# Partial-array matmuls alternate between row halves, column halves and quadrants, and each join step writes one bank

## The chip, the core and the metric

The kernel runs on one core of one Trainium2 chip. The metric is the device time of one execution in microseconds; lower is better. Three executions of the kernel before took 2127.93, 2128.15 and 2136.32 us, so the time before is their median, 2128.15 us.

## What is computed

The reference is one sequence of 256 tokens of width 1024 through two blocks. The first block has two layers of feed-forward, a mixer of three kinds of heads, a cross attention to a memory, and a second feed-forward. The second block has a gated delta rule over a context and then over the tokens, an attention, and a convolved feed-forward. Two places of it matter here. The RWKV heads of the mixer run a recurrence that the kernel solves in two chunks of 128 tokens:

```python
sa = jnp.einsum('bhij,bhj->bhi', state, -kk_t)
state = (state * w_t[:, :, None, :] + sa[..., None] * (kk_t * a_t)[:, :, None, :]
         + v_t[..., None] * k_t[:, :, None, :])
```

and the gated delta rule solves a triangular system per chunk:

```python
a_mat = jnp.where(strict, beta[..., :, None] * dec * kk, 0.0) + jnp.eye(GDN_CHUNK, dtype=jnp.float32)
uw = lax.linalg.triangular_solve(a_mat, rhs, left_side=True, lower=True, unit_diagonal=True)
```

Both come down to inverses of 128x128 unit triangular matrices, eight at a time. The mixer also holds two small attentions with heads of 64 (`foxmoba`), whose scores contract over 64 rows.

## The kernel before

**What fills TensorE.** Most of the program is large products in a three-term split (`xh*wh + xl*wh + xh*wl`, with `h` and `l` the rounded value and its rest). They come from `gemm_pair` (moving tiles of 256 columns) and `gemm_tok` (512 columns). Weights arrive through `raw`, ScalarE makes `wh`, VectorE makes `wl`. Every matmul is recorded on line 351, every transpose on line 354, so tiles are told apart by name.

**What runs beside them.** `merge` and `Side` interleave several generators: each `yield t` hands the turn to whichever generator is due next. In the mixer these are two RWKV groups (`rwkv` with `gi` 0 and 1), `foxmoba` and `mix_out`. During the feed-forwards after the first mixer, the context side of the delta rule (`context`) runs beside them; in the second block the token side does. A scheduler then places the instructions on each engine, mostly in the order in which they were written. TensorE takes its queue in that order as far as waits go.

**The inverse.** `inverse` (line 676) is called 12 times: 4 in the mixers (`rN`, `rW`), 4 for the context and 4 for the tokens (`gN`, `gW`, in two of the last `xv` in place of `gW`). It takes eight matrices in two halves `hf` of four. `lows` says for each half whether it is lower or upper triangular: both lower in the mixers, one of each in the delta rule. After a 16x16 stage on VectorE and a step on the whole array there are four join steps, called A to D here. A and B work on 32x32 quadrants of the array, C and D on 64x64 quarters:

- A multiplies a block of `N` with one of `T` into `Z`, 16 matmuls;
- B multiplies `Z` with `W`, 16 matmuls, and 8 more (`own`) that give the transposed block;
- C and D do the same on 64x64, 8 matmuls each.

An fp32 matmul leaves two records in the trace, so an inverse has 112 records of TensorE in A to D (80 on quadrants, 32 on quarters). Before the change, each half and each pair of blocks `(ee, oo)` has a bank of its own (`ps = e.bank()`, out of two) and an evacuation of its own, and its four matmuls on one quadrant stand in a row:

```python
for hf, (ee, oo) in eo:
    ps = e.bank()
    for j in range(4):
        u = 4 * hf + j
        s.mm(ps[qd(oo), j * 32:j * 32 + 32], N[qd(ee), u, qd(oo)], T[qd(ee), u, qd(ee)])
    s.act(Z[qd(oo), hs[hf], :32], v4(ps[qd(oo), :128]))
```

**The other places.** `scores` in `foxmoba` contracts over 64 rows, head by head, two heads per row half. In `rwkv`, `inv` makes `N` from four matmuls on the low row half and then four on the high one; `rest` makes `G` with two matmuls per head, four heads, heads alternating between row halves with a `yield 1.5` after each; the loop over chunks at its end multiplies `U` and `vt` with `G` on column halves; `values` in `foxmoba` also works on column halves.

Of the kernel before, what the change touches and what calls it, by code (L numbers as in the profile page):

```python
# [189 lines left out]
def f2(ap):  # L190
    return ap.rearrange("p a b -> p (a b)")
# [84 lines left out]
class Builder:  # L276
# [399 lines left out]
    def inverse(s, e, N, W, lows, pace=(1.0, 1.0)):  # L676
# [75 lines left out]
        for hf, (ee, oo) in eo:  # L752

            ps = e.bank()
            own = (ee < 2) == lows[hf]
            for j in range(4):
                u = 4 * hf + j
                s.mm(ps[qd(ee), j * 32:j * 32 + 32], Z[qd(oo), u, :32], W[qd(oo), u, qd(oo)])
            if own:
                for j in range(4):  # L760
                    u = 4 * hf + j
                    s.mm(ps[qd(oo), j * 32:j * 32 + 32], W[qd(oo), u, qd(oo)], Z[qd(oo), u, :32])
                nc.vector.tensor_copy(T[qd(oo), hs[hf], qd(ee)], v4(ps[qd(oo), :128]))
            s.act(W[qd(ee), hs[hf], qd(oo)], v4(ps[qd(ee), :128]))
        yield 1.5 * pace[1]

        for hf, sl in enumerate(hs):
            a, b = (slice(0, 64), slice(64, 128)) if lows[hf] else (slice(64, 128), slice(0, 64))
            ps = e.bank()
            for j in range(4):  # L770
                u = 4 * hf + j
                s.mm(ps[b, j * 64:j * 64 + 64], N[a, u, b], T[a, u, a])
            s.act(Z[b, sl, :64], v4(ps[b, :256]))
        yield 1.5 * pace[1]
        for hf, sl in enumerate(hs):
            a, b = (slice(0, 64), slice(64, 128)) if lows[hf] else (slice(64, 128), slice(0, 64))
            ps = e.bank()
            for j in range(4):
                u = 4 * hf + j
                s.mm(ps[a, j * 64:j * 64 + 64], Z[b, u, :64], W[b, u, b])  # L780
            s.act(W[a, sl, b], v4(ps[a, :256]))
        yield 1.5 * pace[1]


# [102 lines left out]
    def foxmoba(s, e, l, m):  # L887
# [32 lines left out]
        for a in range(2):  # L920
# [56 lines left out]
            def scores(qb):  # L977
                n = 128 * (qb + 1)
                sc = e.t([128, 4, 256], "fcb" if a and qb else "sc")[:, :, :n]
                for p in range(2):  # L980
                    ps = e.bank()
                    for i in range(2):
                        h = 2 * i + p
                        o = ps[:, i * n:i * n + n]
                        rw = slice(64 * p, 64 * p + 64)
                        s.mm(o, qT[rw, i, qb * 128:qb * 128 + 128], qT[rw, 2 + i, :n])
# [20 lines left out]
            def values(qb, sc):  # L1007
                PT = e.t([128, 2, 4, 128], "PT")
                for kb in range(qb + 1):
                    pt = e.bank()  # L1010
                    for h in range(4):
                        s.tr(pt[:, h * 128:h * 128 + 128], sc[:, h, kb * 128:kb * 128 + 128])
                    s.act(f2(PT[:, kb]), pt)
                yield 2.0
                po = e.bank()
                for i in range(2):
                    for p in range(2):
                        h = 2 * i + p
                        vc = slice(a * 256 + h * 64, a * 256 + h * 64 + 64)
                        o = po[64 * p:64 * p + 64, i * 128:i * 128 + 128]  # L1020
                        for kb in range(qb + 1):
# [18 lines left out]
    def rwkv(s, e, ec, l, gi, m):  # L1040
# [79 lines left out]
        def inv():  # L1120
# [1 line left out]
                yield "inv0"  # L1122
            N = t([128, 8, 128], "rN")
            nc.gpsimd.memset(N, 0.0)
            for p in range(2):
                ps = e.bank()
                rw = slice(64 * p, 64 * p + 64)
                for c in range(2):
                    cc = slice(c * 128, c * 128 + 128)
                    for ct in range(2):  # L1130
                        u = c * 2 + ct
                        s.mm(ps[:, u * 128:u * 128 + 128], nb[rw, ct, cc], E[rw, 0, ct, cc])
# [6 lines left out]
        def rest():  # L1139
# [60 lines left out]
        for c in range(2):  # L1200
# [31 lines left out]
            for ct in range(2):  # L1232
                o = ps[:, ct * 128:ct * 128 + 128]
                if c:
                    s.mm(o, SB[:, ct], E[:, 1, ct, cc], ct == 0, False)
                for pr in range(2):
                    h = 2 * ct + pr
                    hc = slice(h * 64, h * 64 + 64)
                    oo = o[64 * pr:64 * pr + 64]
                    s.mm(oo, U[:, hc], G[:, h, 0], ct == 0 and not c, False)  # L1240
                    s.mm(oo, vt[:, c, hc], G[:, h, 2], False, ct == 1)
            s.act(y[:, :, cc], v2(ps[:, :256]))
            flags.add(f"scan{gi}{c}")
            yield 2.0
# [825 lines left out]
```

## Time and profile before

| | before |
|---|---|
| median of 3 runs | 2128.15 us |
| profiled execution, its own time | 2126.08 us |
| span in the trace | 2124.3 us |
| mean granted TensorE clock | 0.97 of full speed |
| TensorE busy | 2040.3 us (96%) |
| VectorE busy | 1606.1 us (76%) |
| ScalarE busy | 1128.2 us (53%) |

The span runs from the first to the last instruction of the profiled execution; 1.8 us of its own time lie around it, and that time is 2.1 us below the median. A row of the timeline gives the start, the length from the first start to the last end, the engine, the line, the operation, the tiles it writes and reads, and how many records it merges. The end of a matmul is modelled and reaches past the start of the next one, so what a matmul costs TensorE is the distance from start to start, not its length.

### The profile page before, as it was taken

The page shows a single profiled execution, that of the slowest core. Times are in us where ns is not written, and L with a number is a line of the kernel's source. Part 1 is how long each engine was busy: PE and PEld are TensorE (multiplying, and loading weights), DVE is VectorE, ACT ScalarE, POOL GpSimd, SP SyncE. Part 2 cuts the span into 40 slices and gives each one's busy share as a digit, 9 for nine tenths or more (in the row PEclk, how much of TensorE's full clock was granted, in tenths as well). Part 3 has the DMA queues.
Part 4 walks back from the last instruction along what each step waited for, and adds up shares of the span by engine and source line. Part 5 has one row for each costly group of instructions (what it writes and reads, how often), then busy time and mean ns, then how long its engine had stood idle before and what let it go on. Part 6 is the DMA issues. An engine that isn't in the chain of part 4 may idle for free.

```text
span 2124.3 us, 37334 instructions
## 1 busy us (share of the span) xinstructions
PE 2040.3 (96%) x14344; PEld 1802.5 (85%) x14344; DVE 1606.1 (76%) x3832; ACT 1128.2 (53%) x2113; POOL 14.9 (1%) x16
## 2 busy tenths in 40 slices
PE   8999999999999999999999978999889999999998
PEld 8899887778989989898888768999678888878996
DVE  7977688477695969586698578686788787767985
ACT  6544554376454556464555355444546564546663
POOL 0000000000000000000000000000000000000000
PEclk9999999899999999999999898999989999999999
DMA  8766532154554445454432167665431123555564
GB/s 300 243 225 179 158 108 70 53 171 129 163 160 147 155 135 161 148 163 141 147 119 80 43 216 246 197 226 170 136 98 60 51 61 100 168 163 166 197 191 129
DMA packets 90570, 317.18 MB, mean 149 GB/s; under 512 B 10388, under 2 KB 12952, under 8 KB 90008
## 3 DMA queue, kind: packets, MB, share of 16 engines
q1 hardware_dynamic: 90392, 314.80, 46.7%
q8 instruction: 112, 1.84, 0.4%
q14 instruction: 66, 0.54, 0.1%
HBM read 313.72 MB, written 1.05 MB: 148 GB/s over the span
## 4 chain that ended last, share of the span: by engine, by line
PE 78%; DVE 15%; ACT 3%; issue 2%; DMA 1%; SPq 0%; ACTq 0%; DVEq 0%
PE b L351 75%; DVE wl L327 4%; PE b L354 4%; ACT wh L324 1%; DVE iv_x L348 1%; DVE macc L345 1%; DVE iv_tz L701 1%; DVE iv_p L327 1%; DMA wm<-in_wmod_dram 1%; DVE gcv L345 1%; ACT sq L324 1%; ACT iv_c L324 0%; DVE sg L327 0%; DVE iv_tz L327 0%; DVE gW L327 0%
## 5 line engine op out<-in xcount | busy, mean ns | idle before, releaser
L324 ACT ACTIVATE wh<-raw 128x1024 fp32r<-128x1024 f32 (+1 forms) x546 | 568.9, 1043 | 602.6 <-PE b L351 443.1
L327 DVE TENSOR_TENSOR wl<-raw,wh 128x1024 fp32r<-128x1024 f32 (+1 forms) x546 | 654.2, 1201 | 266.1 <-ACT wh L324 234.4
L351 PE MATMUL b<-xTh,wh 128*128 128x256 f32 x2200 | 625.7, 285 | 2.9 <-ACT xTh L324 2.4
L351 PE MATMUL b<-xTh,wl 128*128 128x256 f32 x2200 | 621.1, 283 | 1.2 <-DVE wl L327 1.2
L351 PE MATMUL b<-xTl,wh 128*128 128x256 f32 x2200 | 620.4, 283 | 0.3 <-DVE xTl L345 0.2
L351 PEld LDWEIGHTS b<-xTh,wh 128*128 128x128 f32 x2200 | 416.6, 190 | 8.5 <-ACT xTh L324 3.9
L351 PEld LDWEIGHTS b<-xTh,wl 128*128 128x128 f32 x2200 | 417.6, 190 | 3.6 <-DVE wl L327 1.9
L351 PEld LDWEIGHTS b<-xTl,wh 128*128 128x128 f32 x2200 | 417.7, 190 | 3.1 <-DVE xTl L345 1.3
L351 PE MATMUL b<-wh,gh 128*128 128x512 f32 x440 | 176.0, 400 | 0.2 <-DVE gcv L345 0.2
L351 PE MATMUL b<-wl,gh 128*128 128x512 f32 x440 | 174.5, 397 | 0.2 <-DVE wl L327 0.2
L351 PE MATMUL b<-wh,gl 128*128 128x512 f32 x440 | 173.8, 395 | 0.0
L351 PE MATMUL b<-wh,xTh 128*128 128x512 f32 x400 | 163.1, 413 | 6.3 <-DVE iv_x L348 5.0
L351 PE MATMUL b<-wl,xTh 128*128 128x512 f32 x400 | 163.8, 411 | 0.3 <-DVE wl L327 0.3
L351 PE MATMUL b<-wh,xTl 128*128 128x512 f32 x400 | 162.4, 407 | 0.0
L351 PEld LDWEIGHTS b<-wl,gh 128*128 128x128 f32 x440 | 83.5, 190 | 18.6 <-DVE wl L327 0.6
L351 PEld LDWEIGHTS b<-wh,gh 128*128 128x128 f32 x440 | 83.5, 190 | 18.3 <-ACT wh L324 0.6
L351 PEld LDWEIGHTS b<-wh,gl 128*128 128x128 f32 x440 | 83.5, 190 | 17.3
L351 PEld LDWEIGHTS b<-wh,xTh 128*128 128x128 f32 x400 | 76.4, 192 | 25.4 <-issue 8.6
L351 PEld LDWEIGHTS b<-wl,xTh 128*128 128x128 f32 x400 | 76.9, 192 | 19.7 <-issue 4.0
L351 PEld LDWEIGHTS b<-wh,xTl 128*128 128x128 f32 x400 | 77.0, 192 | 15.6 <-issue 1.0
L345 DVE SCALAR_TENSOR_TENSOR macc<-wm,mcs,macc 128x512 f32<-128x512 f32 x112 | 82.6, 747 | 0.8 <-DMA wm<-in_wmod_dram 0.3
L324 ACT ACTIVATE iv_tz<-b 32x128 f32<-32x128 f32 (+2 forms) x96 | 31.1, 325 | 62.0 <-PE b L351 58.2
(608 smaller groups left out, 3181.3 us busy)
## 6 DMA issues: line engine op xcount, KB each, us to landing
raw<-in_f1i_dram SPq DMA_DIRECT2D x88, 512.0 KB, 3.8
raw<-in_f2i_dram SPq DMA_DIRECT2D x88, 512.0 KB, 4.2
wm<-in_wmod_dram SPq DMA_DIRECT2D x48, 512.0 KB, 4.8
raw<-in_wup_dram SPq DMA_DIRECT2D x44, 512.0 KB, 4.4
raw<-in_f1o_dram SPq DMA_DIRECT2D x40, 512.0 KB, 3.7
raw<-in_wi_q_dram SPq DMA_DIRECT2D x40, 512.0 KB, 3.8
raw<-in_f2o_dram SPq DMA_DIRECT2D x40, 512.0 KB, 3.7
raw<-in_wi_a_dram SPq DMA_DIRECT2D x32, 512.0 KB, 3.9
```

The costliest lines, as they stand in the source:

```text
L324: return s.nc.scalar.activation(out, in_, func, scale=scale, bias=bias, **kw)
L327: return s.nc.vector.tensor_tensor(out, a, b, op=op)
L345: return s.nc.vector.scalar_tensor_tensor(out, a, sc, b, op0=op0, op1=op1)
L348: s.nc.vector.tensor_reduce(out, in_, axis=AX.X, op=op)
L351: s.last_mm = s.nc.tensor.matmul(out, lhsT, rhs, start=start, stop=stop).ins
L354: s.nc.tensor.transpose(out, in_, s.c("ident"))
L701: nc.vector.stream_shuffle(AR[:, j, :, j:], NC[:, :, j:], [j] * 16 + [16 + j] * 16)
```

## The change

The matmuls of A to D are written in another order: the loop over `j` is outside, so that neighbours in the queue stand on different quadrants or quarters, and a whole step writes one bank. `alike` is true in the mixers, where both halves use the same quadrants and the second half then takes other columns of the bank. In the delta rule the halves use different quadrants and share columns. Fewer, larger evacuations follow: step A has 2 instead of 4 (`alike`) or 1, step C has 1 instead of 2. `own` of step B gets a bank apart. `N`, `G`, `scores`, the products with `G` and `values` alternate in the same way, with their banks as before; `G` goes by pairs of heads with a `yield 3.0`.

```diff
-        for hf, (ee, oo) in eo:
-            ps = e.bank()
-            for j in range(4):
-                u = 4 * hf + j
-                s.mm(ps[qd(oo), j * 32:j * 32 + 32], N[qd(ee), u, qd(oo)], T[qd(ee), u, qd(ee)])
-            s.act(Z[qd(oo), hs[hf], :32], v4(ps[qd(oo), :128]))
+        alike = lows[0] == lows[1]
+        co = lambda hf, w: 4 * w * hf if alike else 0
+        ps = e.bank()
+        for j in range(4):
+            for hf, (ee, oo) in eo:
+                u, c = 4 * hf + j, co(hf, 32) + 32 * j
+                s.mm(ps[qd(oo), c:c + 32], N[qd(ee), u, qd(oo)], T[qd(ee), u, qd(ee)])
+        if alike:
+            for oo in sorted({oo for _, (_, oo) in eo}):
+                s.act(Z[qd(oo), :, :32], ps[qd(oo), :256].rearrange("p (a b) -> p a b", a=8))
+        else:
+            s.act(Z[:, :4, :32], v4(ps[:, :128]))
...
+        own = [(hf, q) for hf, q in eo if (q[0] < 2) == lows[hf]]
+        ps = e.bank()
+        for j in range(4):
+            for hf, (ee, oo) in eo:
+                u, c = 4 * hf + j, co(hf, 32) + 32 * j
+                s.mm(ps[qd(ee), c:c + 32], Z[qd(oo), zu(hf, j), :32], W[qd(oo), u, qd(oo)])
+        po = e.bank()
+        for j in range(4):
+            for hf, (ee, oo) in own:
+                u, c = 4 * hf + j, co(hf, 32) + 32 * j
+                s.mm(po[qd(oo), c:c + 32], W[qd(oo), u, qd(oo)], Z[qd(oo), zu(hf, j), :32])
...
+        ps = e.bank()
+        for j in range(4):
+            for hf, (a, b) in enumerate(ab):
+                u, c = 4 * hf + j, co(hf, 64) + 64 * j
+                s.mm(ps[b, c:c + 64], N[a, u, b], T[a, u, a])
...
+                pp = [e.bank() for _ in range(2)]
+                for i in range(2):
+                    for p in range(2):
+                        rw = slice(64 * p, 64 * p + 64)
+                        s.mm(pp[p][:, i * n:i * n + n], qT[rw, i, qb * 128:qb * 128 + 128], qT[rw, 2 + i, :n])
...
-                for h in range(4):
-                    ct, rw = h // 2, slice(64 * (h % 2), 64 * (h % 2) + 64)
-                    ps = ec.bank()
-                    s.mm(ps[:, :128], nb[rw, ct, cc], E[rw, 1, ct, cc])
-                    s.mm(v2(ps[:, 128:384]), kt[rw, ct, cc], E[rw, 0:2, ct, cc])
-                    nc.vector.copy_predicated(f2(G[:, h]), s.uc[:, 640:1024], ps[:, :384])
-                    yield 1.5
+                for ct in range(2):
+                    pp = [(ec.bank(), slice(64 * p, 64 * p + 64)) for p in range(2)]
+                    for ps, rw in pp:
+                        s.mm(ps[:, :128], nb[rw, ct, cc], E[rw, 1, ct, cc])
+                    for ps, rw in pp:
+                        s.mm(v2(ps[:, 128:384]), kt[rw, ct, cc], E[rw, 0:2, ct, cc])
+                    for p, (ps, rw) in enumerate(pp):
+                        nc.vector.copy_predicated(f2(G[:, 2 * ct + p]), s.uc[:, 640:1024], ps[:, :384])
+                    yield 3.0
```

What this does to the queue of TensorE is shown at three places. First, steps A and B of the first context inverse, before (`gN` is `N`, `gW` is `W`, `iv_tz` holds `T` and `Z`; the `128x256` rows are the large product that fills the time, one of several each time):

```order
L351 MATMUL b_7046<-iv_tz,gN 32x32 x4
L351 MATMUL b_7052<-iv_tz,gN 32x32 x4
L351 MATMUL b_7070<-xTh,wh 128x256
...
L351 MATMUL b_7058<-iv_tz,gN 32x32 x4
L351 MATMUL b_7064<-iv_tz,gN 32x32 x4
...
L351 MATMUL b_7101<-gW,iv_tz 32x32 x4
L351 MATMUL b_7101<-iv_tz,gW 32x32 x4
L351 MATMUL b_7112<-gW,iv_tz 32x32 x4
...
L351 MATMUL b_7118<-gW,iv_tz 32x32 x4
L351 MATMUL b_7070<-xTl,wh 128x256
L351 MATMUL b_7124<-gW,iv_tz 32x32 x4
L351 MATMUL b_7124<-iv_tz,gW 32x32 x4
```

and the same two steps on TensorE after the change:

```order
L351 MATMUL b_7018<-iv_tz,gN 32x32 x16
L351 MATMUL b_7036<-xTh,wh 128x256
L351 MATMUL b_7036<-xTl,wh 128x256
...
L351 MATMUL b_7036<-xTh,wl 128x256
L351 MATMUL b_7067<-gW,iv_tz 32x32 x16
L351 MATMUL b_7084<-iv_tz,gW 32x32 x8
```

Five stretches of quadrant matmuls became two; between A and B stand 24 matmuls of the large product, and C and D (not shown) are one stretch of 8 matmuls each, as they were. Second, TensorE in the first mixer where the inverse of the second RWKV group joins, before (`rE`, `ra`, `rzk` belong to `G`, `wl` and `wh` with `xTh` to the large product):

```order
L351 MATMUL b_4073<-iv_tz,rN 32x32 x4
L351 MATMUL b_4135<-rE,ra 128x128
L351 MATMUL b_4079<-iv_tz,rN 32x32 x4
L351 MATMUL b_4135<-rE,rzk 128x256
L351 MATMUL b_4085<-iv_tz,rN 32x32 x4
L351 MATMUL b_4091<-iv_tz,rN 32x32 x4
L351 MATMUL b_4152<-wl,xTh 128x512
L351 MATMUL b_4152<-wh,xTh 128x512
L351 MATMUL b_4101<-rW,iv_tz 32x32 x4
L351 MATMUL b_4101<-iv_tz,rW 32x32 x4
```

and after (`rG`, `rU`, `rvt`, `rSB` are the products with `G` at the end of the first group):

```order
L351 MATMUL b_4059<-iv_tz,rN 32x32 x14
L351 MATMUL b_4115<-rG,rvt 64x128
L351 MATMUL b_4115<-rE,rSB 128x128
L351 MATMUL b_4115<-rG,rU 64x128
L351 MATMUL b_4086<-rW,iv_tz 32x32
L351 MATMUL b_4115<-rG,rU 64x128
L351 MATMUL b_4115<-rG,rvt 64x128
L351 MATMUL b_4086<-rW,iv_tz 32x32 x15
L351 MATMUL b_4103<-iv_tz,rW 32x32 x8
```

The join steps are now whole, and less of the large product stands between them. Third, `scores` over 256 keys on TensorE in the first mixer, before (two banks, `b_4451` and `b_4456`, one for each row half):

```order
L351 MATMUL b_4451<-qkT 128x256
L351 MATMUL b_4456<-qkT 128x256
L351 MATMUL b_4462<-wl,xTh 128x512
L351 MATMUL b_4463<-wh,xTl 128x512
L351 MATMUL b_4451<-qkT 128x256
L351 MATMUL b_4487<-fconst,rE_3111 128x2
L351 MATMUL b_4456<-qkT 128x256
```

and after:

```order
L351 MATMUL b_4423<-qkT 128x256
L351 MATMUL b_4424<-qkT 128x256
L351 MATMUL b_4423<-qkT 128x256
L351 MATMUL b_4424<-qkT 128x256
L351 MATMUL b_4459<-fconst,rE_3111 128x2 x4
```

The four matmuls of the scores now follow each other. Over the whole program, TensorE's 12552 matmuls are the same ones; neighbours that differ in the part of the array they use in size (whole, half, quarter, quadrant) are 380 pairs before and 318 after.

## Rows read from the trace of the kernel before

**Rows 1.** The page: span, busy time by engine, the chain by engine.
```profile
span 2124.3 us, 37334 instructions
...
PE 2040.3 (96%) x14344; PEld 1802.5 (85%) x14344; DVE 1606.1 (76%) x3832; ACT 1128.2 (53%) x2113; POOL 14.9 (1%) x16
...
PE 78%; DVE 15%; ACT 3%; issue 2%; DMA 1%; SPq 0%; ACTq 0%; DVEq 0%
```

**Rows 2.** Stretches: length, busy by engine (records), granted clock, DMA share, GB/s.
```profile
300.00:445.00 145.00, 142.97 (x1020) 110.52 (x1019) 96.26 (x266) 67.21 (x157) 3.72 (x3) 0.93 0.25 82
640.00:1005.00 365.00, 357.18 (x2975) 333.73 (x2974) 274.42 (x640) 194.46 (x363) 0.00 (x0) 0.99 0.48 150
...
1580.00:1800.00 220.00, 211.73 (x1703) 188.83 (x1703) 173.14 (x600) 123.78 (x301) 0.00 (x0) 0.93 0.21 66
```

**Rows 3.** Stretches of single inverses, PE's `iv_tz` matmuls alone; last: all twelve.
```profile
368.70:388.10 19.40, 8.28 (x112) 0.53 0.04 6
...
651.00:668.00 17.00, 4.86 (x112) 1.00 0.53 170
...
1653.00:1667.00 14.00, 6.54 (x112) 0.76 0.24 77
...
sum 189.00, PE 71.92; mean PE 5.99
```

**Rows 4.** Timeline, PE: four matmuls on one quadrant, between large ones.
```profile
309.36 0.28 PE L351 MATMUL b<-xTh,wh 128*128 128x256 f32 x1
309.56 0.43 PE L351 MATMUL b<-iv_tz,rN 32*32 32x32 f32 x8
309.93 0.39 PE L351 MATMUL b<-xTl,wh 128*128 128x256 f32 x1
310.15 0.28 PE L351 MATMUL b<-xTh,wl 128*128 128x256 f32 x1
```

**Rows 5.** Timeline, PE: half of step A, two quadrants in two banks.
```profile
653.00 0.28 PE L351 MATMUL b<-xTh,wl 128*128 128x256 f32 x1
653.21 0.59 PE L351 MATMUL b<-iv_tz,gN 32*32 32x32 f32 x16
653.73 0.39 PE L351 MATMUL b<-xTh,wh 128*128 128x256 f32 x1
```

**Rows 6.** Timeline, PE: step C, two quarters in two banks.
```profile
662.77 0.28 PE L351 MATMUL b<-xTl,wh 128*128 128x256 f32 x1
662.89 0.28 PE L351 MATMUL b<-xTh,wl 128*128 128x256 f32 x1
663.10 0.96 PE L351 MATMUL b<-iv_tz,gN 64*64 64x64 f32 x16
```

**Rows 7.** Timeline, PE: start of step B.
```profile
655.31 0.34 PE L351 MATMUL b<-gW,iv_tz 32*32 32x32 f32 x5
655.46 0.21 PE L351 MATMUL b<-iv_tz,gW 32*32 32x32 f32 x1
655.49 0.19 PE L351 MATMUL b<-gW,iv_tz 32*32 32x32 f32 x1
```

**Rows 8.** Timeline, PE: `G`, two heads that stand together, then one alone.
```profile
328.07 0.50 PE L351 MATMUL b<-rE,ra 64*128 64x128 f32 x4
328.39 0.61 PE L351 MATMUL b<-rE,rzk 64*128 64x256 f32 x4
...
331.86 0.49 PE L351 MATMUL b<-rE,ra 64*128 64x128 f32 x2
332.19 0.59 PE L351 MATMUL b<-rE,rzk 64*128 64x256 f32 x2
```

**Rows 9.** Timeline, PE: `N` of the first group, two row halves.
```profile
266.98 1.71 PE L351 MATMUL b<-rE,ra 64*128 64x128 f32 x16
```

**Rows 10.** Timeline, PE: scores over 256 keys, both halves, then one.
```profile
419.22 0.70 PE L351 MATMUL b<-qkT 64*128 64x256 f32 x4
...
420.52 0.70 PE L351 MATMUL b<-qkT 64*128 64x256 f32 x2
```

More of the change, by code (lines that the diff above doesn't have):

```diff
@@ L765, in inverse @@
-        yield 1.5 * pace[1]
[L767 to L773, printed above, removed]
-        yield 1.5 * pace[1]
[L775 to L781, printed above, removed]
+        alike = lows[0] == lows[1]
@@ new lines, in inverse @@
+        zu = lambda hf, j: 4 * hf + j if alike else j
+        yield 1.5 * pace[1]
+        own = [(hf, q) for hf, q in eo if (q[0] < 2) == lows[hf]]
[9 more added lines that the diff above has]
+                s.mm(po[qd(oo), c:c + 32], W[qd(oo), u, qd(oo)], Z[qd(oo), zu(hf, j), :32])
@@ new lines, in inverse @@
+        if alike:
+            for hf, (ee, oo) in own[:1]:
+                nc.vector.tensor_copy(T[qd(oo), :, qd(ee)], po[qd(oo), :256].rearrange("p (a b) -> p a b", a=8))
+            for hf, (ee, oo) in eo[:2]:
+                s.act(W[qd(ee), :, qd(oo)], ps[qd(ee), :256].rearrange("p (a b) -> p a b", a=8))
+        else:
+            for hf, (ee, oo) in own:
+                nc.vector.tensor_copy(T[qd(oo), hs[hf], qd(ee)], v4(po[qd(oo), :128]))
+            for hf, (ee, oo) in eo:
+                s.act(W[qd(ee), hs[hf], qd(oo)], v4(ps[qd(ee), :128]))
@@ new lines, in inverse @@
+        yield 1.5 * pace[1]
+        ab = [(slice(0, 64), slice(64, 128)) if low else (slice(64, 128), slice(0, 64)) for low in lows]
+        ps = e.bank()
[3 more added lines that the diff above has]
+                s.mm(ps[b, c:c + 64], N[a, u, b], T[a, u, a])
+        if alike:
+            s.act(Z[ab[0][1], :, :64], ps[ab[0][1]].rearrange("p (a b) -> p a b", a=8))
+        else:
+            s.act(Z[:, :4, :64], v4(ps[:, :256]))
@@ L782, in inverse @@
+        yield 1.5 * pace[1]
+        ps = e.bank()
+        for j in range(4):
+            for hf, (a, b) in enumerate(ab):
+                u, c = 4 * hf + j, co(hf, 64) + 64 * j
+                s.mm(ps[a, c:c + 64], Z[b, zu(hf, j), :64], W[b, u, b])
+        if alike:
+            a, b = ab[0]
+            s.act(W[a, :, b], ps[a].rearrange("p (a b) -> p a b", a=8))
+        else:
+            for sl, (a, b) in zip(hs, ab):
+                s.act(W[a, sl, b], v4(ps[a, :256]))
         yield 1.5 * pace[1]
@@ L1016, in values @@
                 for i in range(2):
[L1017 to L1021, printed above, removed]
+                    for kb in range(qb + 1):
+                        for p in range(2):
+                            h = 2 * i + p
+                            vc = slice(a * 256 + h * 64, a * 256 + h * 64 + 64)
+                            o = po[64 * p:64 * p + 64, i * 128:i * 128 + 128]
                             s.mm(o, v[:, kb, vc], PT[:, kb, h], kb == 0, kb == qb)
@@ L1124, in inv @@
             nc.gpsimd.memset(N, 0.0)
[L1125 to L1132, printed above, removed]
+            pp = [e.bank() for _ in range(2)]
+            for c in range(2):
+                cc = slice(c * 128, c * 128 + 128)
+                for ct in range(2):
+                    u = c * 2 + ct
+                    for p in range(2):
+                        rw = slice(64 * p, 64 * p + 64)
+                        s.mm(pp[p][:, u * 128:u * 128 + 128], nb[rw, ct, cc], E[rw, 0, ct, cc])
+            for p, ps in enumerate(pp):
                 nc.vector.copy_predicated(N[:, 4 * p:4 * p + 4], s.uc[:, 512:640][:, None, :].to_broadcast([128, 4, 128]), v4(ps))
@@ L1170, in rest @@
                 nc.gpsimd.memset(G, 0.0)
-                for h in range(4):
-                    ct, rw = h // 2, slice(64 * (h % 2), 64 * (h % 2) + 64)
-                    ps = ec.bank()
-                    s.mm(ps[:, :128], nb[rw, ct, cc], E[rw, 1, ct, cc])
-                    s.mm(v2(ps[:, 128:384]), kt[rw, ct, cc], E[rw, 0:2, ct, cc])
-                    nc.vector.copy_predicated(f2(G[:, h]), s.uc[:, 640:1024], ps[:, :384])
-                    yield 1.5
+                for ct in range(2):
+                    pp = [(ec.bank(), slice(64 * p, 64 * p + 64)) for p in range(2)]
[6 more added lines that the diff above has]
+                    yield 3.0
                 st["G"].append(G)
@@ L1235, in rwkv @@
                     s.mm(o, SB[:, ct], E[:, 1, ct, cc], ct == 0, False)
[L1236 to L1241, printed above, removed]
+                for k, first in ((0, ct == 0 and not c), (2, False)):
+                    for pr in range(2):
+                        h = 2 * ct + pr
+                        hc = slice(h * 64, h * 64 + 64)
+                        s.mm(o[64 * pr:64 * pr + 64], vt[:, c, hc] if k else U[:, hc], G[:, h, k], first, k == 2 and ct == 1)
             s.act(y[:, :, cc], v2(ps[:, :256]))
```

17 lines of the change are left out of this document (1 added, 16 removed).

## The prediction

> **What bounds the kernel now.** I read the page first, then busy time by stretch, then the timeline of TensorE at the places that the diff touches. TensorE is busy for 2040.3 of 2124.3 us and holds 78% of the chain that ended last; VectorE has 15% of it [rows 1]. By stretch the picture is the same: in the first mixer 143.0 of 145.0 us, where the context inverses run 357.2 of 365.0 us, in the second block, with the token inverses, 211.7 of 220.0 us [rows 2]. So what TensorE saves is time saved in the mixers and the context part nearly in full; in the second block less, since TensorE waits there for 8 us. VectorE and ScalarE have room (76% and 53%), so the fewer evacuations are not the gain. The clock matters in one way: in the inverse that ends the first mixer and in some token inverses the granted clock is 0.53 and 0.76 of full [rows 3], that is, part of the stretch runs at 1.2 GHz instead of 2.4, although TensorE has work there. The same records cost more at these places.
>
> **Prices.** One stretch on a part of the array between large matmuls: from 309.36 to 310.15 there are 0.79 us, and two large matmuls without it would take about 0.12 us each [rows 4, 6]. The stretch costs 0.55 us. Its eight records last 0.43 us, and the first five of a like stretch 0.34 us [rows 4, 7], so a record on one quadrant takes (0.43 - 0.34)/3 = 0.03 us; eight are 0.25 us, and **0.30 us is the price of leaving the whole array and coming back**. Part of it is the entry: 0.21 us from the last large matmul to the first small one in place of 0.12 [rows 5].
>
> Sixteen records on two quadrants last 0.59 us [rows 5], only 0.16 us or five records more than eight on one. Since four matmuls on one quadrant stand ahead of four on the other in the queue, TensorE has started the second quadrant while the first still had three records to go. Rows 7 show it: after five records of the first tile comes one of the second, though eight of the first stand ahead of it. Two heads of `G` that stand together take 0.50 and 0.61 us, one head alone 0.49 and 0.59 [rows 8], and in the queue the second head's first record is four behind the first head's first. So TensorE starts records on another part up to about four records ahead, and written in turn two parts run fully side by side. For a quarter I take (0.96 - 0.19)/13 = 0.06 us per record: 0.96 us is the length [rows 6], 0.19 us that of a single record [rows 7], and 13 steps are what sixteen records took on two quadrants.
>
> **The change part by part.** *Context inverses (4).* Before: A is two stretches, B three, C and D one each, so seven at 0.30 = 2.1 us. The records: A twice 0.59 - 0.19 = 0.8 us; C and D twice 0.96 - 0.19 = 1.5 us; B is what is left of 4.86 us [rows 3] after 1.18 and 1.92, less 0.19 for each of its three stretches, 1.2 us. Together 5.6 us. After: four stretches, 1.2 us. A's 32 records stand on four quadrants in turn: eight steps if all four run side by side (0.25 us), 32 if none do (1.0 us); no row shows four, and I take ten steps, 0.3 us, near the lower end because two and two kinds [rows 5, 7, 8] overlap whenever the queue lets them. B's 48 records by the same count 18 steps, 0.55 us (ends 0.5 and 1.5); C and D 8 to 9 steps each, 1.0 us (ends 0.9 and 1.8). Sum 3.1 us, so 2.5 us less each and **10 us for four**; with no overlap 5.5, 0.1 us less each.
>
> *Token inverses (4).* All twelve hold 71.9 us of records' time; without the four at 4.86 us the mean is 6.6 us [rows 3], because they are cut into some nine stretches and part of the time is at the lower clock. With 9 times 0.30 less 9 times 0.19 they cost 7.6 us. After: 3.1 us over a clock of 0.76 [rows 3], 4.1, and one more stretch, 4.4. That is 3.2 us each, 13 us; TensorE waits in this block and not all of it is on the path, so two thirds: **9 us**.
>
> *Inverses of the mixers (4).* Both halves use the same quadrants, so A alternates between two, and C and D stay on one quarter. C and D gain only the second stretch. For the first group I get 7.2 us before (ten stretches) and 5.2 after (six), 2.0 us each for two; for the second group, 8.3 us of records at a clock of 0.53 [rows 3], 1.5 us each, since less of the large product now covers its evacuations. **7 us.**
>
> *The rest.* `N`: sixteen records in 1.71 us [rows 9] are thirteen steps of 0.11 and a last one; in turn they are eight or nine, 0.5 us less, four times: **2 us**. Scores: four records on two halves last as long as two on one [rows 10]; four scores over 256 keys could give 1.2 us each, but part already ran beside `G`: **3 us**. `G`: in the new queue ten of 32 heads still stand alone, before twelve; two times 0.9 us [rows 8]: **2 us**. `values` and the products with `G` on column halves already alternated within four records: nothing; were they to lose overlap, 1 us.
>
> *What it adds.* One evacuation now waits for the last of 16 matmuls, and the next step's first matmul waits for it at the head of TensorE's queue, with the large product and all transposes behind it. In the context inverses 24 large matmuls, 2.7 us, cover this. In the second group of each mixer and in the token inverses only one to four matmuls do; at six inverses, four steps and some 0.2 us I charge **4 us** (from 0, if the evacuation is in time, to 0.6 us per step, 14). Fewer ScalarE instructions I cost at nothing: ScalarE is at 53%.
>
> Sum: 10 + 9 + 7 + 2 + 3 + 2 - 4 = 29 us. The profiled execution took 2126.1 us (2124.3 of span), so 2097; the median of the runs is 2.1 us above that execution, so I predict **2099 us**.
>
> **Rivals.** *Strictly in program order.* If TensorE began every record in the order of the queue, a tile's second record would hold up the next tile, and a matmul would take one step and a few ns, not half a step. Each inverse would give 0.6 us less and the sum 22 us: 2106 us. Rows 7 and 8 speak against it. The Trainium skill's page "TensorE: Matmul & The Clock Gate" (Part 3) says that matmuls keep program order in start and end and that only weight loads are pulled ahead; by it the time would be this one, and the trace disagrees in the starts (0.15 us into a stretch whose first tile needs 0.25).
>
> *Row parts that share a bank take turns.* Before, different row quadrants always wrote different banks; now all of A, and `ps` of B, C and D, write one. No row of before shows two row parts in one bank at a time; rows 7 show only column parts of the same rows. If the second had to wait, A to D would gain nothing from alternating and keep only the fewer stretches: 0.1 us for each context inverse, 1 to 2 us in all for the token ones, 3 us in the mixers, and 7 us from `N`, scores and `G`, whose banks are apart; with half of the waits, 9 us: 2119 us. The Trainium skill's page "TensorEngine Tiling (Array Packing)" (Restrictions and Gotchas, PSUM pressure) says that different row tiles cannot access one bank at the same time. It speaks against this change, and by it the time is this one.
>
> *Each turn is paid for.* If going from one quadrant to the next at every matmul cost the entry of a stretch, 0.21 - 0.12 = 0.09 us [rows 5], the some 50 turns in each of 12 inverses and 100 elsewhere would cost 63 us; the fewer stretches (31 of about 176) give 10 back: 2181 us, slower. It decides from about 0.015 us a turn if nothing overlaps. Against it: in rows 7 tiles change at every record 0.03 us apart.
>
> *The stretches were filler.* If the chain in the second block and at the ends of the mixers is the inverse's own way through VectorE and ScalarE, TensorE only waits longer: 10 us of the 29 stay out, 2109 us; with the evacuations at 0.6 us too, 2119 us.
>
> **How the numbers follow.** My forecast has 0.57; program order 0.10, the shared bank 0.16, the price of a turn 0.07, filler 0.10. The range from 2084 (four quadrants fully side by side, the half-clock stretches shorter too) to 2122 leaves out the slow case and some of the shared bank. A measurement can tell about 0.5%, 10.6 us, from no change; faster is below 2117.5. Faster: nearly all of the forecast and program order, three quarters of filler, a third of the shared bank, 0.72; same: the rest of these, 0.20; slower: 0.08.
>
> **What will show it.** The context inverses: four stretches, and the `iv_tz` records of one in about 2.5 us instead of 4.86; A's 32 records within 0.5 us if four quadrants run side by side, 1.2 us if the bank is shared in turn. `N` in 1.2 us. No new waits of TensorE for ScalarE in the second block. Wrong would be a busy time that falls by 30 us with idle time that grows by as much, or steps of 0.1 us from record to record.

## The result, and the profile after

The kernel after takes **2097.39 us** (median of four executions, 2094.68 to 2102.34); the kernel before took 2130.10 us in the same comparison (2127.93 to 2136.32). The ratio is **0.9835, 95% interval 0.9807 to 0.9864**. The prediction was 2099 us, 2084 to 2122. The profiled execution of after took 2097.77 us. One execution of a later kernel (order alone, 2149.09 us) was slow and is left out of that kernel's ratio and means.

The page of after (span, busy time by engine), against [rows 1]:

```profile
span 2095.9 us, 37277 instructions
...
PE 2006.1 (96%) x14344; PEld 1778.8 (85%) x14344; DVE 1604.1 (77%) x3828; ACT 1113.9 (53%) x2057; POOL 14.9 (1%) x16
```

TensorE does the same 14344 records in 34.2 us less; its idle time grows from 84.0 to 89.8 us. Next the first mixer, the context part, the second mixer and the inverses of the second block, cut at the same large matmuls in both kernels; first before, then after (columns as in [rows 2]):

```profile
205.50:439.60 234.10, 229.94 (x1539) 185.40 (x1538) 162.28 (x471) 117.14 (x251) 7.35 (x6) 0.96 0.32 100
439.60:1036.50 596.90, 585.17 (x4385) 534.14 (x4383) 450.21 (x1065) 330.56 (x623) 1.98 (x2) 0.99 0.48 153
1036.50:1236.40 199.90, 195.70 (x1385) 157.65 (x1384) 147.66 (x450) 102.10 (x228) 5.38 (x5) 0.96 0.29 91
1525.40:1815.80 290.40, 273.07 (x2069) 241.78 (x2068) 230.74 (x770) 161.93 (x373) 0.00 (x0) 0.94 0.25 77
```

```profile
206.40:431.70 225.30, 216.77 (x1539) 176.47 (x1538) 163.14 (x469) 114.87 (x239) 7.31 (x6) 0.99 0.33 104
431.70:1017.00 585.30, 572.05 (x4383) 524.33 (x4382) 449.64 (x1065) 324.92 (x607) 1.88 (x2) 0.99 0.50 156
1017.00:1220.90 203.90, 197.91 (x1386) 160.83 (x1385) 148.08 (x449) 100.42 (x216) 5.48 (x5) 0.93 0.29 91
1510.20:1786.70 276.50, 258.96 (x2069) 229.01 (x2068) 228.71 (x770) 157.41 (x357) 0.00 (x0) 0.96 0.26 81
```

The context part gives 11.6 us, the second block 13.9, the first mixer 8.8; the second mixer takes 4.0 us more. The granted clock goes with the odd ones: 0.96 to 0.99 in the first mixer, 0.96 to 0.93 in the second. Where the clock is even, in the context part (13.7 us at half clock in both traces), the gain is work alone. There, the four steps of the first context inverse on TensorE (timeline, of B the first records), which answer to [rows 5 to 7]:

```profile
639.96 0.45 PE L351 MATMUL b<-iv_tz,gN 32*32 32x32 f32 x32
...
643.29 0.42 PE L351 MATMUL b<-gW,iv_tz 32*32 32x32 f32 x28
...
649.58 0.68 PE L351 MATMUL b<-iv_tz,gN 64*64 64x64 f32 x16
...
653.13 0.68 PE L351 MATMUL b<-gW,iv_tz 64*64 64x64 f32 x16
```

All 32 records of A last 0.45 us, about as long as eight on one quadrant did before (0.43), where half of A took 0.59; C and D take 0.68 in place of 0.96 us. The sum for this inverse, TensorE's `iv_tz` records alone ([rows 3] has 4.86 us):

```profile
639.00:655.00 16.00, 2.52 (x112) 1.00 0.61 194
```

`N` and the scores over 256 keys, in the first mixer of after ([rows 9, 10]):

```profile
268.56 1.16 PE L351 MATMUL b<-rE,ra 64*128 64x128 f32 x16
...
408.00 1.36 PE L351 MATMUL b<-qkT 64*128 64x256 f32 x8
```

`N` went from 1.71 to 1.16 us; the scores' eight records now take 1.36 us in one stretch, where they took three of some 0.62 us each, counted to the start of the next matmul ([rows 10] have two of them). But ten us later TensorE has longer waits than in the kernel before, which waits only ahead of the first of three groups (the bracket is the idle time and what ended it; first before, then after):

```profile
428.97 0.66 PE L351 MATMUL b<-PT,fmv 128*64 128x128 f32 x8 [0.25 <-ACT PT L324]
```

```profile
418.54 0.66 PE L351 MATMUL b<-PT,fmv 128*64 128x128 f32 x8 [0.79 <-ACT PT L324]
419.88 1.53 PE L354 MATMUL b<-fconst,fcb 128*128 128x128 f32 x4 [0.69 <-ACT fcb L324]
421.87 0.84 PE L351 MATMUL b<-wh,xTh 128*128 128x512 f32 x2 [0.46 <-ACT xTh L324]
```

The three of after stand at the end of the second mixer too. With others, the idle time of TensorE in the two mixers rises from 8.4 to 14.5 us (length less busy time in the rows above).

### The profile page after: what moved, and what is told of

Read it like the earlier page. It is cut to its first block, busy times and chain, and to the rows that moved or that the text cites. A ratio compares the mean times of both kernels' runs of the same rounds, so it can differ in the third digit from the quotient of the medians.

```text
span 2095.9 us, 37277 instructions
## 1 busy us (share of the span) xinstructions
PE 2006.1 (96%) x14344; PEld 1778.8 (85%) x14344; DVE 1604.1 (77%) x3828; ACT 1113.9 (53%) x2057; POOL 14.9 (1%) x16
## 4 chain that ended last, share of the span: by engine, by line
PE 77%; DVE 16%; ACT 4%; issue 2%; DMA 0%; SPq 0%; DVEq 0%; ACTq 0%
PE b L351 73%; DVE wl L327 4%; PE b L354 3%; ACT wh L324 1%; DVE iv_x L348 1%; DVE iv_tz L701 1%; DVE iv_p L327 1%; DVE macc L345 1%; DVE gcv L345 1%; DVE sg L327 1%; ACT sq L324 1%; ACT iv_c L324 0%; DVE iv_tz L327 0%; DVE sg L345 0%; ACT fcb L324 0%
## 5 line engine op out<-in xcount | busy, mean ns | idle before, releaser
L351 PEld LDWEIGHTS b<-wh,gl 128*128 128x128 f32 x440 | 83.3, 189 | 17.1
L351 PEld LDWEIGHTS b<-wh,xTl 128*128 128x128 f32 x400 | 76.6, 191 | 16.5 <-issue 2.3
L324 ACT ACTIVATE iv_tz<-b 128x256 f32<-128x256 f32 (+3 forms) x52 | 19.7, 380 | 66.0 <-PE b L351 65.7
```

The lines of the kernel that those rows point to most:

```text
L324: return s.nc.scalar.activation(out, in_, func, scale=scale, bias=bias, **kw)
L351: s.last_mm = s.nc.tensor.matmul(out, lhsT, rhs, start=start, stop=stop).ins
```

## The experiments

**The price of a stretch, by itself.** A kernel that only measures: small fp32 matmuls between large ones. A tile is row quadrant, column quadrant and bank; `turn` changes the tile at every matmul, `rows` after four:

```python
...
("two_same", 32, turn([(0, 1, 0), (2, 3, 0)], 8)),
("two_apart", 32, turn([(0, 1, 0), (2, 3, 1)], 8)),
("two_fours", 32, rows([(0, 1, 0), (2, 3, 0)], 8)),
...
```

> Nothing of the reference is computed (the output is zeros). Fifteen stretches of small fp32 matmuls stand between runs of 16 large ones of 128x256, three times over; each names its own operand: one matmul (one_s), four (one_m) and sixteen (one_q) on one quadrant; sixteen on two quadrants in turn in one bank (two_same), in two banks (two_apart), by fours in a row (two_fours); sixteen on four quadrants in turn in one bank (four_same), in four banks (four_apart), by fours (four_fours); two quadrants of the same rows (two_cols), two of the same columns in two banks (two_rows); eight 64x64 on one quarter (one_h), on two in turn in one bank (h_same), in two (h_apart), by fours (h_fours). Theory, as the cost of a stretch beyond the large matmuls: a price of 0.30 us plus 0.03 us for each record that isn't covered: one_s 0.35, one_m 0.55, one_q 1.25; two_same and two_apart alike 0.8, two_fours 1.0 to 1.1; four_same and four_apart alike 0.55 to 0.6, four_fours 0.9 to 1.0; one_h 1.25, h_same and h_apart 0.8, h_fours 1.05. Rival A (row parts that share a bank take turns): two_same and four_same cost what one_q costs, 1.25, and only two_apart and four_apart are short. Rival B (each turn is paid for): four_same costs more than four_fours.

Timeline of TensorE (`big` are the large matmuls), one row of the first of three alike rounds and then the second:

```profile
46.71 1.14 PE L79 MATMUL b<-one_h 64*64 64x64 f32 x16
...
58.33 0.24 PE L79 MATMUL b<-one_s 32*32 32x32 f32 x2
58.50 2.17 PE L71 MATMUL b<-big 128*128 128x256 f32 x16
60.60 0.43 PE L79 MATMUL b<-one_m 32*32 32x32 f32 x8
60.97 2.17 PE L71 MATMUL b<-big 128*128 128x256 f32 x16
63.06 1.19 PE L79 MATMUL b<-one_q 32*32 32x32 f32 x32
64.19 2.17 PE L71 MATMUL b<-big 128*128 128x256 f32 x16
66.28 0.69 PE L79 MATMUL b<-two_same 32*32 32x32 f32 x32
66.91 2.17 PE L71 MATMUL b<-big 128*128 128x256 f32 x16
69.00 0.69 PE L79 MATMUL b<-two_apart 32*32 32x32 f32 x32
...
71.72 0.89 PE L79 MATMUL b<-two_fours 32*32 32x32 f32 x32
...
74.64 0.45 PE L79 MATMUL b<-four_same 32*32 32x32 f32 x32
75.03 2.17 PE L71 MATMUL b<-big 128*128 128x256 f32 x16
77.12 0.45 PE L79 MATMUL b<-four_apart 32*32 32x32 f32 x32
...
79.60 0.89 PE L79 MATMUL b<-four_fours 32*32 32x32 f32 x32
...
82.52 0.69 PE L79 MATMUL b<-two_cols 32*32 32x32 f32 x32
```

From the start of a stretch to the next large matmul, two records take 0.17 us, eight 0.37 and 32 take 1.13: (1.13 - 0.37)/24 = 0.032 us a record on one quadrant. Two quadrants in turn take half (0.63), four a quarter (0.39 with its way out); `two_cols`, two quadrants of the same rows, as much as two of different rows. One bank or several makes no difference, and neither does a change of quadrant at every record. Counted from the large matmul before to the second one behind, and less the usual 0.12 us each, a stretch of two records costs 0.365 us; without 2 times 0.032 the price of leaving the array and coming back is 0.30 us. On one quarter a record takes (1.14 - 0.21)/15 = 0.062 us. In fours two quadrants take 0.83 us (the length less 0.06, as in the other rows), between 1.13 (all on one quadrant) and 0.63: the second is started ahead, but only a few records. Four quadrants in fours take no less (0.89 us of length, as two).

So the prices of the prediction hold, and rivals A and B fall. The Trainium skill's page "TensorEngine Tiling (Array Packing)" (Restrictions and Gotchas, PSUM pressure) has different row tiles barred from one bank at one time; with the column quadrants apart, as here, the trace shows no such thing (0.69 us in one bank and in two, 0.45 in one and in four).

**Order and banks apart.** The new `inverse` alone (all else as before) twice, and its two halves. `e3_banks` has the new banks and evacuations with the old order (its difference from the new `inverse` at each of the steps):

```diff
-        for j in range(4):
-            for hf, (ee, oo) in eo:
+        for hf, (ee, oo) in eo:
+            for j in range(4):
```

`e4_order` has the old banks, evacuations and stretches, and alternates inside them (the head of step A):

```diff
-        for hf, (ee, oo) in eo:
-            ps = e.bank()
-            for j in range(4):
+        for hf in range(2):
+            two = [(e.bank(), q) for h, q in eo if h == hf]
+            for j in range(4):
+                for ps, (ee, oo) in two:
```

> Only the function `inverse` is changed as in the kernel after (order, banks, evacuations); N, G, scores, values and the products with G stay as before. Theory (the prediction's terms): the inverses carry 22 to 26 of the 29 us, so 26 us less than the kernel before, about 2104 us. Rival A (the trace of after shows the second mixer 4 us slower than before, so the other edits gave nothing there or cost something): all of the gain is in the inverses, 2098 us or less. Rival B (the half-clock stretch of 23.9 us in the second mixer of after comes from the new order of the inverses): it shows here too, and the second mixer is slower than before here as well.

> In `inverse`, banks and evacuations as in the kernel after (one bank per step, whole stretches), but the four matmuls of one quadrant or quarter stand in a row as before; everything else as before. Theory (neighbouring records on other parts run side by side up to about four records ahead): a context or token inverse loses 13 steps of 0.03 us in A, 18 in B and some 4.5 of 0.06 in C and D against the alternating order, 1.5 us, eight times; 0.4 us in four mixer inverses: 13 to 14 us slower than the run with the whole new inverse, about 2117 us; the records of step A of a context inverse then take 0.7 us and not 0.3. Rival (fewer stretches and evacuations are the gain, the order within them is not): as fast as with the whole new inverse, 2104 us.

> In `inverse`, alternating order inside the old stretches: two quadrants of one half in A and in B, the two quarters in C and D, each tile with its own bank and its own evacuations as before, so as many stretches and as many evacuations as before. Theory: 13 steps become 8 to 9 in two stretches each of A and B (0.14 us each) and in C and D (0.27 us each), 1.1 us for each of eight inverses and 0.6 for four in the mixers: 11 us less than before, about 2119 us. Rival (fewer stretches and evacuations are the gain): nothing, 2130 us.

> The new inverse alone, once more, since four executions left an interval of 1.1%. If the other edits give anything beside the new inverse, this is slower than the kernel after by 3 to 8 us; if they give nothing or cost through the clock, it is as fast or faster.

Measured against the kernel before: the new inverse alone 2100.19 us, 0.9848 (0.9791 to 0.9905), and again 2101.05 us, 0.9857 (0.9827 to 0.9887); banks alone 2132.82 us, 1.0004 (0.9977 to 1.0032); order alone 2137.35 us, 0.9998 (0.9960 to 1.0037). The new inverse alone lies between the 2104 us forecast and the 2098 of rival A; rival B falls, since its second mixer takes 199.7 and 198.1 us in the two traces against 199.9 before. The first context inverse, `iv_tz` records of TensorE, in the order banks, order, both:

```profile
643.00:664.00 21.00, 4.02 (x112) 1.00 0.50 159
```

```profile
658.00:676.00 18.00, 3.90 (x112) 1.00 0.52 173
```

```profile
649.00:666.00 17.00, 2.53 (x112) 1.00 0.60 185
```

In the inverse each theory is met nearly to the digit: banks without the order 1.49 us worse than both (1.5 expected), order alone 0.96 better than before (1.1 expected). Step A of `e3_banks` shows why:

```profile
646.88 0.89 PE L351 MATMUL b<-iv_tz,gN 32*32 32x32 f32 x32
```

0.89 us for what takes 0.45 in turn. And yet the times of the two halves are those of the kernel before: they were forecast 16 and 18 us too low. In the trace of the banks alone the context part is 5.0 us shorter than before (591.9 us, clock 0.99), but the two mixers are 10.8 us longer, with 68 us at half clock against 38. What took the gain back is in the main the clock, below.

**The rest alone.** `N`, `G`, scores, values and products alternate, `inverse` is the old one.

> The rest alone: N, G, scores, values and the products with G alternate as in the kernel after, `inverse` is that of before. Theory: N 2, scores 3, G 2 us, so 7 us less than the kernel before, about 2123 us, all of it between 235 and 445 us and between 1030 and 1245 us of the span. Rival A: nothing, within 2 us of the kernel before, because what N and the scores save was covered by work beside them or by waits that grow. Rival B: slower than before by up to 4 us, if the new stalls of TensorE ahead of the matmuls of values (0.8 us, twice) cost more than the scores give.

2138.54 us, 1.0033 (1.0001 to 1.0065): the expected 7 us are not there. Rival B has the sign. The waits of `values` are there (0.69 us and 0.46 behind it, at the end of both mixers), but they are too small for the whole of it; see next.

**The clock.** Each execution has its span and its mean granted clock. Span times clock is the time that would be left if each us at half clock (1.2 GHz) counted half; the remainder is lost to the clock. It is bookkeeping, not pure work: where TensorE waits anyway a low clock costs less. Means over all timed executions:

| kernel | executions | span | full clock | lost |
|---|---|---|---|---|
| before | 41 | 2130.1 | 2062.8 | 67.3 |
| rest alone | 10 | 2135.7 | 2054.7 | 81.0 |
| banks alone | 10 | 2129.6 | 2046.5 | 83.1 |
| order alone | 9 | 2129.6 | 2056.3 | 73.4 |
| new inverse | 8 | 2097.2 | 2042.7 | 54.5 |
| after | 8 | 2094.8 | 2046.3 | 48.5 |

The means are uncertain by about 1 us in the fourth column and 1 to 4 in the fifth. By this count every part does less work, the banks alone 16 us less, but the three parts lose 6 to 16 us more than before to the clock, and the two kernels with the whole new inverse 13 to 19 us less.

The count overstates the clock. Among the executions of one kernel, each us more in the last column goes with only 0.75 us more of span (0.70 to 0.79 in each of the six kernels, 86 executions). At that price, an estimate, the gain of 35.3 us from before to after is 21 us of work and 14 of clock; the banks alone do 12 us less work and pay 12 for the clock, the order alone 5 and 5, the rest alone 5 and 10, the new inverse alone gains 23 and 10. Forecast were 13, 11, 7 and 26 of work.

To see where, the kernel after, the rest and the banks were traced again.

> The kernel after, unchanged, beside the kernel before on this chip. What it tells apart: how much of the gain is less work of TensorE and how much a higher mean clock. Taking span times granted clock as the time at full clock, 25 executions of the kernel before have 2063 of a mean span of 2129 us (66 us lost to the clock), the runs with the new inverse alone 2042 (53 us lost). Theory: the kernel after needs 2035 to 2042 us at full clock (the sum of what the inverse and the rest give alone, 21 and 8 us, or less where they cover the same waits) and loses 50 to 55 us to the clock, 2090 to 2097 us. Rival (the stretch of 23.9 us at half clock in the second mixer belongs to this kernel): it is in this profile at the same place.

> The new banks with the old order once more, for a second trace. In the first trace 68 us of the mixers (230 to 445 and 1030 to 1245 us) ran at half clock, 55 of them in the second, against 38 in the trace of before. Theory (whether the clock falls at an inverse of a mixer differs from run to run of one kernel): the places differ between the two traces by at least one inverse that falls in one and not in the other. Rival (it belongs to this order of the work): the same three inverses fall for about as long.

> The rest alone once more, for a second trace. In the first trace all four inverses of the mixers fell to half clock, 92 us. Theory (differs from run to run): at least one of the four doesn't fall here. Rival (it belongs to this order of the work): all four fall again, for 80 to 100 us.

After again: 2095.95 us, 0.9829 (0.9783 to 0.9874), with 2047.4 us at full clock and 46.1 lost, so longer at full clock and less lost than the 2035 to 2042 and 50 to 55 expected; rest again 2137.59 us and banks again 2149.74 us, one execution each. The four inverses of the mixers in turn (first and second group of the first, then of the second mixer), 25 us from the start of each; the granted clock is the third number from the end. First the trace of after, then of after again:

```profile
306.00:331.00 25.00, 24.91 (x272) 21.51 (x274) 18.32 (x46) 11.08 (x24) 0.95 (x1) 1.00 0.27 85
366.00:391.00 25.00, 25.00 (x230) 18.54 (x229) 12.87 (x33) 8.54 (x16) 1.38 (x1) 1.00 0.09 29
1085.00:1110.00 25.00, 24.15 (x194) 22.34 (x195) 11.43 (x27) 7.44 (x15) 0.95 (x1) 0.56 0.22 67
1157.00:1182.00 25.00, 25.00 (x229) 18.49 (x229) 12.94 (x33) 8.51 (x16) 1.38 (x1) 1.00 0.09 29
```

```profile
307.00:332.00 25.00, 24.25 (x195) 22.05 (x196) 12.06 (x31) 6.23 (x13) 0.95 (x1) 0.57 0.21 64
378.00:403.00 25.00, 25.00 (x202) 17.79 (x201) 8.04 (x17) 5.30 (x11) 1.38 (x1) 0.72 0.03 6
1108.00:1133.00 25.00, 24.67 (x271) 21.89 (x271) 18.27 (x44) 12.20 (x25) 0.95 (x1) 1.00 0.27 87
1169.00:1194.00 25.00, 25.00 (x230) 18.45 (x229) 12.94 (x33) 8.46 (x16) 1.38 (x1) 1.00 0.09 28
```

and of the rest alone, second trace:

```profile
305.00:330.00 25.00, 24.69 (x216) 22.07 (x218) 11.92 (x33) 8.25 (x21) 0.95 (x1) 0.73 0.20 61
370.00:395.00 25.00, 25.00 (x200) 19.06 (x199) 10.05 (x27) 5.43 (x16) 1.38 (x1) 0.70 0.07 22
1107.00:1132.00 25.00, 24.68 (x206) 22.00 (x207) 12.63 (x34) 8.45 (x20) 0.95 (x1) 0.70 0.21 65
1176.00:1201.00 25.00, 25.00 (x199) 19.11 (x199) 9.89 (x27) 5.43 (x16) 1.38 (x1) 0.69 0.08 23
```

Both theories have a share. The first group's inverse of a mixer falls in one execution and not in the next of the same kernel (0.56 in the second mixer in one trace of after, 0.57 in the first mixer in the other), so the 4.0 us that the second mixer seemed to lose belong to that execution (it takes 193.4 us in the other); the banks alone fell in the first group of the first mixer only in the second trace. But much stays from trace to trace: all four fall in both traces of the rest (92 and 65 us at half clock), the three that fell under the banks alone fell again, and the second group's inverse fell in all 16 cases of the kernel before and of the kernels with a part of the change, and in three of ten in the kernels that hold the whole change (after twice, and the three below). Why just the whole keeps the second group at full clock is **not settled**: what the edits change there is how matmuls on parts of the array and the few large ones follow each other.

**Filling the waits.** TensorE waits 0.8 to 3.3 us ahead of ten of the inverses; idle matmuls stand there now.

```diff
+            if not hf:
+                p0 = e.bank()
+                for _ in range(fill):
+                    s.mm(p0[:, 256:], a[:, 0], s.c("tri"))
```

> The kernel after with 30 idle matmuls of 128x256 (0.43 us each, 13 us in all, results unused) ahead of the first matmul of ten of the twelve inverses, where TensorE waits 0.8 to 3.3 us for VectorE (some 17 us in all). Theory (TensorE's idle time there brings the clock down for the inverse that follows): the half-clock stretches that start within 35 us of these places, 54 of 112 us in the profile of after, shrink by more than half, which gives 13 us or more, less some 3 us for idle matmuls that don't fit into the waits: 10 us less than the kernel after. Rival (it is the small matmuls of the inverse and of what runs beside it that let the clock fall): the half-clock stretches stay, and it is 2 to 4 us slower than the kernel after.

2103.02 us, 0.9831 (0.9769 to 0.9892): as fast as after, not 10 us faster. But the waits are not filled. The idle matmuls read `a[:, 0]`, which VectorE writes as well, so most of the waiting now stands ahead of them. At the last context inverse, in after and then here:

```profile
950.80 1.40 PE L351 MATMUL b<-iv_tz,gN 128*128 128x64 f32 x8 [3.27 <-DVE iv_tz L327]
```

```profile
952.77 3.04 PE L351 MATMUL b<-fconst,gW 128*128 128x256 f32 x8 [2.20 <-DVE gW L327]
```

At the ten places together TensorE still waits 13.2 us, against 17.1 in after. The half-clock stretches that begin between such a wait and 35 us behind an inverse's first matmul are 41 us, against 54 and 68 in the two traces of after; the mean loss is 45.1 us against 48.5 over four executions, within the spread, and the time at full clock is 4 us more. So this run hardly tests the theory or its rival. For the second groups, at least, idle time isn't needed: in the rows of the rest alone above they fall to 0.70 and 0.69 while TensorE is busy for all of the 25.00 us.

**A step further.** If four quadrants in turn cost 8 ns a record, the two whole-array steps ahead of A can be done by blocks too (the first of them, without the lines around it):

```diff
-                s.mm(ps[:, j * 64:j * 64 + 64].rearrange("p (b i) -> p b i", i=16), N[:, 4 * hf + j], odd(T[:, 4 * hf + j], hf))
+        for u in range(8):
+            for b in range(4):
+                c = 32 * b if lows[u // 4] else 32 * b + 16
+                s.mm(ps[qd(b), u * 16:u * 16 + 16], N[qd(b), u, qd(b)], T[qd(b), u, c:c + 16])
```

> A step further, on top of the kernel after: the two whole-array steps of an inverse that stand before step A (16 matmuls of 128x64 each, 32 records of 0.11 us in the two together) are written as matmuls of 32x32 blocks on the diagonal, 32 per step, 16 columns each, on four quadrants in turn in one bank; only the diagonal blocks were used of the old results. Theory: as with four quadrants in turn (8 ns a record, 0.30 us for leaving the whole array), a step costs 64 times 0.008 and 0.3, 0.8 us in place of 1.8; 2.0 us less per inverse, twelve times 24 us, of which I expect four fifths in the total, since TensorE waits in the second block: 19 us less than the kernel after, about 2077 us. Rival A (16 columns on a quadrant overlap less than 32 do): at 0.03 us a record a step costs 2.2 us, 10 us slower than the kernel after. Rival B (less work of TensorE lets the clock fall more, as with the order or the banks alone): the time at full clock falls by 15 us or more and the loss to the clock grows by as much, no change.

> The same, and the eight `own` matmuls of step B stand between its 16 others instead of behind them (other quadrants of the same rows). Theory: two quadrants of the same rows run side by side as two of different rows do, so B's 48 records take 0.25 us less and not more; 0.15 to 0.25 us each, 2 to 3 us in all. Rival: the rest of B waits longer for its evacuations, which now all come at its end: no change, or up to 2 us slower.

2062.45 us, **0.9666** (0.9644 to 0.9688), and with `own` between the rest of B 2056.76 us, **0.9633** (0.9609 to 0.9656). In the first context inverse the two steps took, in after (1.94 us of idle time ahead of the first) and then here:

```profile
624.56 1.07 PE L351 MATMUL b<-iv_tz,gN 128*128 128x64 f32 x8 [1.94 <-DVE iv_tz L327]
...
625.76 1.00 PE L351 MATMUL b<-iv_tz,gN 128*128 128x64 f32 x8
...
631.23 1.89 PE L351 MATMUL b<-iv_tz,gW 128*128 128x64 f32 x16
```

```profile
620.90 0.73 PE L351 MATMUL b<-iv_tz,gN 32*32 32x16 f32 x64 [1.85 <-DVE iv_tz L720]
...
627.46 0.73 PE L351 MATMUL b<-iv_tz,gW 32*32 32x16 f32 x64
```

64 records in 0.73 us: some 8 to 9 ns a record, and rival A falls. In the means of span the gain over after is 34 us and not 19: 32 at full clock (2014.6, four executions, uncertain by 3) and 3 of clock (45.8 lost), so rival B falls too. The 24 us worked out were not to be discounted by a fifth: cut as above, the context part goes from 585.3 to 576.0 us and the second block's inverses from 276.5 to 264.8. Whether the 8 us beyond the 24 are more than the spread, and where they come from, was not followed up. The second version's mean is 4.8 us less again, 4.3 of them clock, and the intervals overlap: the 2 to 3 us expected of `own` are not shown.

## Why the prediction was right, and which steps were not

**The prices** (0.30 us a stretch, 0.03 and 0.06 us a record, starts some four records ahead): shown, with 0.30, 0.032 and, on a quarter, 0.062 us; two quadrants in fours take 0.70 us from the first to the last start (0.89 less the 0.19 us of a record), where 22 steps on one quadrant are 0.70 us and 31 steps 1.0. So each group of four matmuls behind the first costs five steps in place of eight.

**Context inverses, 10 us:** right. The part gives 11.6 us, with the same time at half clock in both; one inverse falls from 4.86 to 2.52 us. Four quadrants run fully side by side, the lower end of the bounds.

**Token inverses, 9 us:** right for the work. The stage gives 13.9 us in one trace and 18.0 in the other of after (290.4 us against 276.5 and 272.4), with 34 us at half clock before and 24 and 10 after. With half of each such us lost and that priced at 0.75, some 10 and 9 us are work; the rest is clock. TensorE's idle time there stays (17.3 and 17.5 us).

**Mixers, 7 us for the inverses and 7 for `N`, scores and `G`:** the step that failed. `N` became 0.55 us shorter, as worked out, and the eight records of the scores at the end of the first mixer 0.5. But the two mixers together took 434.0 us before and 429.2 and 437.0 us in the two traces of after, with 38, 31 and 48 us at half clock; with the clock priced as above they are 1 to 2 us shorter and not 14. That what TensorE saves in the mixers is time saved nearly in full does not hold: TensorE waits 6.1 us more there, some 3.4 at the ends of the mixers and 2.2 in the first one, ahead of large products, for `xTl` and `wl` from VectorE. Where the rest of the missing 12 us went was not followed up. With the rest alone the whole kernel is no faster. Beside the new inverse the rest gives 2.4 us of mean span (2094.8 against 2097.2, each uncertain by 2), which is not clear of nothing, and its time at full clock isn't shorter.

**Evacuations, 4 us charged:** TensorE's waits name no evacuation of a join step. The idle time did grow by 5.8 us, but in the mixers, as just said.

**The sum, 29 us:** right in part by luck, since errors cancel. Over all executions the gain is 35.3 us of span, about 21 of work and 14 of clock (16.5 and 18.8 by the table). The 29 were to be nearly all work, some of it priced at a lower clock: the mixers fell short by some 12, and the evacuations cost less than the 4 charged. For a smaller loss to the clock the sum had no term beyond [rows 3], and why the loss became smaller is open.

**Rivals.** Program order: two quadrants in fours would take four times seven steps of 0.032 us, 0.9 us or more from first to last start, not 0.70. The Trainium skill's page "TensorE: Matmul & The Clock Gate" (Part 3) has matmuls start strictly in program order; this trace disagrees in the starts. The shared bank and the price of a turn fall with the first experiment. "The stretches were filler" holds in part for the mixers, where the waits grew, and not for the context and the second block.

## What to carry to other kernels

Small matmuls on parts of the array belong in whole stretches, in turn over as many different quadrants as there are; order and whole stretches are each worth about 1 us per 112 records here, together 2.3. Ask of each whole-array matmul with a block diagonal operand whether it is such a stretch too: here that was worth about as much again as the change itself (34 us of mean span after 35). Where the granted clock isn't flat, compare work and clock apart, over many executions, with the price of the clock taken from the spread of one kernel, before a part of a change is called worthless.

## What was not expected of the hardware

Two quadrants of the same rows run side by side as fully as two of different rows (0.69 us each). A matmul of 16 columns on a quadrant costs, in turn, as much as one of 32 (64 records in 0.73 us, 32 in 0.45). And the loss to the clock moves by 35 us between kernels whose full-clock times in the table are the same (2046 us), from 48.5 us (after) to 83.1 (banks alone), and in the kernel after from some 35 to 59 us between executions (mean clock 0.983 to 0.972).
